# A Mamba-2 state recurrence inside a hybrid decoder layer: state packed chunk by chunk, stepped from PSUM

## The chip, the cores and the metric

One core of a Trainium2 chip runs the whole layer as one program. The metric is the device time of one execution in microseconds; shown is the median of several executions. The profile of one execution gives the times of single instructions on the engines: TensorE (PE, with its weight loads as PEld), VectorE (DVE), ScalarE (ACT), GpSimd (POOL) and SyncE (SP), which issues DMAs.

## What is computed

One decoder layer over 2048 tokens of width 1024. A joint input projection feeds two groups of heads: an RG-LRU group and a Mamba-2 SSD group; both outputs go through one output projection, and a SwiGLU feed-forward follows. The change lies in the SSD group alone. With 16 heads of 64 channels, a state of 128 and chunks of 128 tokens, the reference computes:

```
a_cs = jnp.cumsum(a, axis=-1)
Lmat = jnp.exp(segsum(a))
scores = jnp.einsum("bclgn,bcsgn->bgcls", Cm, Bm)
y_diag = jnp.einsum("bgecls,bcsgep->bclgep", scores[:, :, None] * Lmat, xs)
decay_states = jnp.exp(a_cs[..., -1:] - a_cs)
states = jnp.einsum("bclgn,bgecl,bclgep->bcgepn", Bm, decay_states, xs)
...
prev_states = jnp.einsum("bgezc,bcgepn->bzgepn", decay_chunk, states)[:, :-1]
y_off = jnp.einsum("bclgn,bcgepn,bgecl->bclgep", Cm, prev_states, jnp.exp(a_cs))
return (y_diag + y_off).reshape(b, t, g, e, p)
```

`prev_states` is a recurrence over chunks: the state ahead of chunk c+1 is the state ahead of chunk c, times the decay of chunk c, plus the chunk's own `states`.

## The kernel before

The sequence is cut in two blocks of 1024 tokens (NB = 2), a block in 8 chunks of 128 (NC = 8). Per block, a loop makes the projections of the input tile by tile: each tile of 128 columns is 48 matmuls of 128x512 (L133, L134, L135), since each fp32 product is made of three products of split operands (`s_hi`, `s_lo` for the weights, `hx` for the activations). Weights are loaded two tiles ahead through SP's queue (L208), rounded by ScalarE (L128) and their remainder taken by VectorE (L129).

The SSD group has 8 tiles `xi` per block, each with two heads (64 columns each), so there are 16 mixes (`ssd_mix`). For each tile `ssd_proj` makes the projections of x and z, with the convolution (L288 to L293) and SiLU (L473 for x, L478 for z). `ssd_mix` is a generator in three parts, which `site` runs between the projections of the next tile:

- Part one: transposes of x (L490), x times dt (`xd`, L492) and times the decay to the chunk's end (`xe`, L494), and the decay matrix `L` (L500 to L502).
- Part two: the states of the 8 chunks, 8 matmuls of 128x128 into one PSUM tile `pst` (L506). ScalarE copies the state from the block before (`sc`) and `pst` into a tile `U` whose chunks lie innermost, [state, column, 9] (L508, L509), and spreads the decays `aet` into a tile `AT` of the same shape (L511). VectorE runs one scan over all 1152 elements (L513), with decay 0 at the first of each nine. The state after the last chunk goes back to `sc` (L516, first block only). `L` is multiplied with the scores `SM` (L517).
- Part three: 8 matmuls with chunk c of `U` as the stationary operand and C as the moving one into `po` (L521), VectorE scales that (L522) and adds the skip (L523); 16 matmuls of the diagonal part into `py` (L527); then sum, gate, and spill to DRAM.

fp32 matmuls show as two passes each, so 8 matmuls are 16 instructions in the trace. PSUM tiles named `pq` come from a pool of two: the transposes L490 of the next mix write the buffer of `po`, which L522 empties. Working tiles `t4` come from a pool of nine. A scheduler places the instructions on the engines by priority in program order; each engine runs its own in order.

Of the kernel before, what the change touches and what calls it, by code (L numbers as in the profile page):

```python
# [8 lines left out]
F32 = mybir.dt.float32  # L9
F32R = mybir.dt.float32r  # L10
AF = mybir.ActivationFunctionType
ALU = mybir.AluOpType
# [3 lines left out]
P = 128  # L16
# [4 lines left out]
NB = T // TB  # L21
HB = 512
NC = TB // P
NH = 16
# [21 lines left out]
def hybrid_layer(ctx: ExitStack, tc: tile.TileContext, x, w_in, pack, heads, rows, wa, wx, w_out, w_gu, w_dn, out):  # L46
    nc = tc.nc
    v, a, te, g, sy = nc.vector, nc.scalar, nc.tensor, nc.gpsimd, nc.sync
# [20 lines left out]
    def par(n, i=0, w=None):  # L69
        o, full = PK[n]  # L70
        return pk[:, o + i:o + i + (w or 1)]
# [65 lines left out]
    def bc(ap, shape):  # L137
        return ap.broadcast_to(shape)

    # ------------------------------------------------ mixers  # L140
    mp = ctx.enter_context(ExitStack())
    pp = mp.enter_context(tc.tile_pool(name="pp", bufs=2, space=PSUM))
    pq = mp.enter_context(tc.tile_pool(name="pq", bufs=2, space=PSUM))
# [112 lines left out]
    with ExitStack() as fr:  # L256
        fc = fr.enter_context(tc.tile_pool(name="fc", bufs=1, reuse_waits="tile"))
        tl = fr.enter_context(tc.tile_pool(name="tl", bufs=1, reuse_waits="tile"))
        tp = fr.enter_context(tc.tile_pool(name="tp", bufs=1, reuse_waits="tile"))
# [11 lines left out]
        def t4(shape=(P, TB)):  # L271
            w = 1
            for n in shape[1:]:
                w *= n
            t = tl.tile([P, P * (NC + 1)], F32, name="t4", bufs=NT4)[:, :w]
            if len(shape) == 3:
                t = t.rearrange("p (a b) -> p a b", b=shape[2])
            elif len(shape) == 4:
                t = t.rearrange("p (a b c) -> p a b c", b=shape[2], c=shape[3])
            return t  # L280

        def wide(name):
            return tp.tile([P, 2, NC, P], F32, name=name, bufs=2)
# [12 lines left out]
        def spill(gt, kt, b):  # L296
            a.dma_start(out=g_dr[b * NC:(b + 1) * NC, :, kt, :].rearrange("c p t -> p c t"),
                        in_=gt.rearrange("p (c t) -> p c t", t=P))

        def accum(gt, sq, acc, first):  # L300
            if first:
                a.activation(out=acc, in_=gt, func=AF.Square)
            else:
                a.activation(out=sq, in_=gt, func=AF.Square)
                v.tensor_add(out=acc, in0=acc, in1=sq)
# [110 lines left out]
        def ssd_dt3(b, dt, dta):  # L416
            sh = [P, NC, NH]
            fl = "p c h -> p (c h)"
            pc = pq.tile([P, 2, 512], F32, name="pq")
            te.matmul(pc[:, 0, 0:P], lhsT=tri, rhs=dta.rearrange(fl), start=True, stop=True)  # L420
            te.matmul(pc[:, 1, 0:P], lhsT=ones, rhs=dta.rearrange(fl), start=True, stop=True)
            pr = pq.tile([P, TB], F32, name="pq")
            for c in range(NC):
                te.matmul(pr[0:NH, c * P:(c + 1) * P], lhsT=dta[:, c, :], rhs=tri, start=True, stop=True)
            cr = tp.tile([P, NC, P], F32, name="Bt", bufs=1).rearrange("p c l -> p (c l)")[0:NH, :]
            v.tensor_copy(out=cr, in_=pr[0:NH, :])
            sy.dma_start(out=cs_dr[b], in_=cr)
            cs = tp.tile(sh, F32, name="cs")
            a.copy(out=cs.rearrange(fl), in_=pc[:, 0, 0:P])
            ed = tp.tile(sh, F32, name="ed")  # L430
            v.tensor_tensor(out=ed.rearrange(fl), in0=pc[:, 1, 0:P], in1=cs.rearrange(fl), op=ALU.subtract)
            a.activation(out=ed, in_=ed, func=AF.Exp)
            aet = tp.tile([P, NH, NC + 1], F32, name="aet")
            v.memset(aet, 0.0)
            a.activation(out=aet[:, :, 1:], in_=pc[:, 1, 0:P].rearrange("p (c h) -> p h c", h=NH), func=AF.Exp)
            return dt, cs, ed, aet

        def ssd_group(b, gi, hT, between):
# [42 lines left out]
        def ssd_mix(b, xi, xc, sz, dts, grp, acc):  # L481
            dt, cs, ed, aet = dts
            C, Bt, SM = grp
            h0 = 2 * xi
            L = wide("L")
            for j in range(2):
                sy.dma_start(out=L[:, j].rearrange("p c l -> p (c l)"), in_=cs_dr[b, h0 + j].partition_broadcast(P))
            pt = pq.tile([P, NC, 2, 64], F32, name="pq")
            for c in range(NC):
                te.transpose(pt[:, c].rearrange("p j d -> p (j d)"), xc[:, c * P:(c + 1) * P], ident)  # L490
            xd = t4((P, NC, 2, 64))
            v.tensor_tensor(out=xd, in0=pt, in1=bc(dt[:, :, h0:h0 + 2, None], [P, NC, 2, 64]), op=ALU.mult)  # L492
            xe = t4((P, NC, 2, 64))
            v.tensor_tensor(out=xe, in0=xd, in1=bc(ed[:, :, h0:h0 + 2, None], [P, NC, 2, 64]), op=ALU.mult)  # L494
            er = t4()
            for j in range(2):
                sy.dma_start(out=er[64 * j:64 * j + 64, :], in_=cs_dr[b, h0 + j].partition_broadcast(64))
            a.activation(out=er, in_=er, func=AF.Exp)
            csb = bc(cs.rearrange("p c h -> p h c")[:, h0:h0 + 2, :, None], [P, 2, NC, P])
            v.tensor_tensor(out=L, in0=L, in1=csb, op=ALU.subtract)  # L500
            v.tensor_scalar(out=L, in0=L, scalar1=0.0, scalar2=None, op0=ALU.min)
            a.activation(out=L, in_=L, func=AF.Exp)  # L502
            yield
            pst = pq.tile([P, NC, P], F32, name="pq")
            for c in range(NC):
                te.matmul(pst[:, c, :], lhsT=Bt[:, c, :], rhs=xe[:, c].rearrange("p j d -> p (j d)"), start=True, stop=True)  # L506
            U = t4((P, P, NC + 1))
            a.copy(out=U[:, :, 0], in_=sc[:, xi, :])  # L508
            a.copy(out=U[:, :, 1:].rearrange("p d c -> p c d"), in_=pst)  # L509
            AT = t4((P, 2, 64, NC + 1))  # L510
            a.copy(out=AT, in_=bc(aet[:, h0:h0 + 2, None, :], [P, 2, 64, NC + 1]))  # L511
            Uf = U.rearrange("p d c -> p (d c)")
            v.tensor_tensor_scan(out=Uf, data0=AT.rearrange("p j d c -> p (j d c)"), data1=Uf,  # L513
                                 initial=0.0, op0=ALU.mult, op1=ALU.add)
            if b + 1 < NB:
                v.tensor_copy(out=sc[:, xi, :], in_=U[:, :, NC])  # L516
            v.tensor_tensor(out=L, in0=L, in1=bc(SM[:, None, :, :], [P, 2, NC, P]), op=ALU.mult)  # L517
            yield
            po = pq.tile([P, NC, P], F32, name="pq")
            for c in range(NC):  # L520
                te.matmul(po[:, c, :], lhsT=U[:, :, c], rhs=C[:, c * P:(c + 1) * P], start=True, stop=True)  # L521
            v.tensor_tensor(out=er, in0=po.rearrange("p c l -> p (c l)"), in1=er, op=ALU.mult)  # L522
            v.scalar_tensor_tensor(out=xc, in0=xc, scalar=par("sd", xi), in1=er, op0=ALU.mult, op1=ALU.add)  # L523
            py = pq.tile([P, NC, P], F32, name="pq")
            for c in range(NC):
                for j in range(2):
                    te.matmul(py[64 * j:64 * j + 64, c, :], lhsT=xd[:, c, j, :], rhs=L[:, j, c, :], start=True, stop=True)  # L527
            v.tensor_tensor(out=xc, in0=py.rearrange("p c l -> p (c l)"), in1=xc, op=ALU.add)
            v.tensor_mul(out=sz, in0=xc, in1=sz)
            spill(sz, 8 + xi, b)  # L530
            accum(sz, xe.rearrange("p c j d -> p (c j d)"), acc, xi == 0)
# [24 lines left out]
        sc = fc.tile([P, 8, P], F32, name="sc")  # L556
# [80 lines left out]
                while stages:  # L637
                    site(3)

    # ------------------------------------------------ output projection  # L640
    def build_op(b, o, halloc, ralloc=raw_tile):
        res = []
        for j in range(2):
            r = ralloc().rearrange("p (k c) -> p k c", c=HB)
            sy.dma_start(out=r, in_=h_dr[b][o][:, 2 * j:2 * j + 2, :])
            for k in range(2):
                hi, lo = halloc(), halloc()
                a.copy(out=hi, in_=r[:, k])
                v.tensor_sub(out=lo, in0=r[:, k], in1=hi.bitcast(F32))  # L649
                res.append((hi, lo))  # L650
        return res
# [26 lines left out]
    with ExitStack() as orr:  # L678
# [36 lines left out]
        for n, t in enumerate(tiles):  # L715
# [34 lines left out]
            b, i, j = t // NC, t % 4, (t % NC) // 4  # L750
# [3 lines left out]
                turn.append(lambda b=b, i=i, j=j, xnt=xnt: turned(b, i, j, xnt))  # L754
    mp.close()

    # ------------------------------------------------ FFN: gate and up
    pf = ctx.enter_context(tc.tile_pool(name="pf", bufs=8, space=PSUM, reuse_waits="tile"))

    def bank():  # L760
# [126 lines left out]
                    for o, z in ((4, s1), (2, s2), (3, s3), (6, s4)):  # L887
                        a.dma_start(out=f_dr[b][o][:, k, :], in_=z)

    # ------------------------------------------------ FFN: down  # L890
    hxs.close()
    with ExitStack() as fb:
        fd = fb.enter_context(tc.tile_pool(name="fd", bufs=1, reuse_waits="tile"))
# [90 lines left out]
        p = prod(0, list(range(2, KF, 2)) + [0], [(2, 0), (2, 1), (2, NB), (4, 0)])  # L984
# [3 lines left out]
        p = prod(2)  # L988
        for t in range(NT):
            v.tensor_add(out=u2[:, t], in0=p[t], in1=m1[:, t])  # L990
        p = prod(3)
        for t in range(NT):
            v.tensor_add(out=u3[:, t], in0=p[t], in1=u2[:, t])
        p = prod(4)
# [5 lines left out]
        p = prod(5)  # L1000
# [10 lines left out]
        p = prod(6)  # L1011
# [54 lines left out]
```

## Time and profile before

| | us |
|---|---|
| median of 3 runs | 2681.18 |
| lowest and highest | 2680.36, 2682.27 |
| span of the profiled execution | 2681.0 |
| TensorE busy in it | 2652.9 |
| VectorE busy | 1803.1 |
| ScalarE busy | 1190.1 |

The profiled execution is as long as the median run, so durations of its rows can be set against the times directly. Busy time of TensorE counts matmuls that overlap in the pipeline, so the chain of work that ended last and the list of waits are read beside it. The two SSD stretches lie at about 90 to 355 us and 600 to 870 us of the span.

### The profile page before, as it was taken

The page shows a single profiled execution, that of the slowest core. Times are in us where ns is not written, and L with a number is a line of the kernel's source. Part 1 is how long each engine was busy: PE and PEld are TensorE (multiplying, and loading weights), DVE is VectorE, ACT ScalarE, POOL GpSimd, SP SyncE. Part 2 cuts the span into 40 slices and gives each one's busy share as a digit, 9 for nine tenths or more (in the row PEclk, how much of TensorE's full clock was granted, in tenths as well). Part 3 has the DMA queues.
Part 4 walks back from the last instruction along what each step waited for, and adds up shares of the span by engine and source line. Part 5 has one row for each costly group of instructions (what it writes and reads, how often), then busy time and mean ns, then how long its engine had stood idle before and what let it go on. Part 6 is the DMA issues. An engine that isn't in the chain of part 4 may idle for free.

```text
span 2681.0 us, 31808 instructions
## 1 busy us (share of the span) xinstructions
PE 2652.9 (99%) x12416; PEld 2206.0 (82%) x12416; DVE 1803.1 (67%) x2460; ACT 1190.1 (44%) x1408; POOL 1.1 (0%) x8
## 2 busy tenths in 40 slices
PE   7999999999999999999999999999999999999998
PEld 5888888878888888888887888888888888888887
DVE  7676777777767777644468776768676766334576
ACT  6554567765554668422244222224222223322443
POOL 0000000000000000000000000000000000000000
PEclk9999999999999999999999999999999999999999
DMA  4333353133223633634355423335333234444664
GB/s 151 103 97 99 94 171 131 47 97 112 91 79 110 210 120 126 227 127 141 130 181 171 151 83 114 103 114 184 111 106 107 96 105 159 147 153 138 220 244 138
DMA packets 186775, 354.39 MB, mean 132 GB/s; under 512 B 18400, under 2 KB 91232, under 8 KB 186624
## 3 DMA queue, kind: packets, MB, share of 16 engines
q1 hardware_dynamic: 85712, 253.16, 28.9%
q10 hardware_dynamic: 100912, 99.20, 10.7%
q8 instruction: 98, 1.61, 0.2%
q14 instruction: 53, 0.43, 0.0%
HBM read 250.45 MB, written 101.84 MB: 131 GB/s over the span
## 4 chain that ended last, share of the span: by engine, by line
PE 94%; DVE 3%; ACT 2%; issue 1%; DMA 1%; SPq 0%; DVEq 0%; ACTq 0%
PE pf L135 16%; PE pf L133 16%; PE pf L134 16%; PE pp L133 11%; PE pp L134 11%; PE pp L135 11%; PE pq L134 3%; PE pq L133 3%; PE pq L135 3%; PE pq L521 2%; PE pq L527 1%; PE pq L506 1%; PE pq L490 1%; PE pq L692 0%; DVE lx L293 0%
## 5 line engine op out<-in xcount | busy, mean ns | idle before, releaser
L133 PE MATMUL pp<-hx,s_hi 128*128 128x512 f32 x1408 | 555.0, 394 | 0.0
L135 PE MATMUL pp<-hx,s_lo 128*128 128x512 f32 x1408 | 551.0, 391 | 0.0
L134 PE MATMUL pp<-hx,s_hi 128*128 128x512 f32 x1408 | 550.3, 391 | 0.6 <-DVE hx L239 0.6
L128 ACT CAST s_hi<-raw 128x1024 fp32r<-128x1024 f32 (+1 forms) x167 | 170.4, 1024 | 318.9 <-PE pq L134 95.0
L135 PEld LDWEIGHTS pp<-hx,s_lo 128*128 128x128 f32 x1408 | 264.9, 188 | 55.8 <-issue 0.2
L134 PEld LDWEIGHTS pp<-hx,s_hi 128*128 128x128 f32 x1408 | 265.3, 188 | 54.7 <-DVE hx L239 1.0
L133 PEld LDWEIGHTS pp<-hx,s_hi 128*128 128x128 f32 x1408 | 265.2, 188 | 54.0 <-issue 0.3
L133 PE MATMUL pf<-hx,s_hi 128*128 128x512 f32 x704 | 274.2, 389 | 0.5 <-ACT s_hi L128 0.5
L135 PE MATMUL pf<-hx,s_lo 128*128 128x512 f32 x704 | 273.9, 389 | 0.7 <-DVE s_lo L129 0.7
L134 PE MATMUL pf<-hx,s_hi 128*128 128x512 f32 x704 | 273.9, 389 | 0.0
L129 DVE TENSOR_TENSOR s_lo<-raw,s_hi 128x1024 fp32r<-128x1024 f32 (+1 forms) x167 | 198.1, 1188 | 97.6 <-ACT s_hi L128 92.3
L909 DVE TENSOR_TENSOR d_lo<-draw,d_hi 128x1024 fp32r<-128x1024 f32 (+1 forms) x110 | 121.4, 1129 | 170.3 <-ACT d_hi L908 170.0
L128 ACT CAST s_hi<-S 128x1024 fp32r<-128x1024 f32 x86 | 90.3, 1050 | 266.6 <-PE pf L134 233.2
L908 ACT CAST d_hi<-draw 128x1024 fp32r<-128x1024 f32 (+1 forms) x110 | 104.8, 980 | 212.4 <-PE pf L134 175.5
L134 PE MATMUL pf<-d_lo,d_hi 128*128 128x512 f32 x504 | 196.1, 389 | 0.0
L135 PE MATMUL pf<-d_hi,d_lo 128*128 128x512 f32 x504 | 195.9, 389 | 0.0
L133 PE MATMUL pf<-d_hi 128*128 128x512 f32 x504 | 194.6, 389 | 0.0
L135 PEld LDWEIGHTS pf<-hx,s_lo 128*128 128x128 f32 x704 | 132.1, 188 | 29.0 <-DVE s_lo L129 1.6
L133 PEld LDWEIGHTS pf<-hx,s_hi 128*128 128x128 f32 x704 | 132.1, 188 | 28.1 <-ACT s_hi L128 0.9
L134 PEld LDWEIGHTS pf<-hx,s_hi 128*128 128x128 f32 x704 | 132.1, 188 | 27.4
L293 DVE SCALAR_TENSOR_TENSOR lx<-xr,pk,lx 128x1024 f32<-128x1024 f32 x108 | 138.2, 1280 | 16.3 <-ACT lx L290 15.4
L134 PE MATMUL pf<-hy,s_hi 128*128 128x512 f32 x356 | 138.8, 390 | 1.5 <-DVE hy L649 1.4
(321 smaller groups left out, 4586.6 us busy)
## 6 DMA issues: line engine op xcount, KB each, us to landing
raw<-w_gu_dram SPq DMA_DIRECT2D x86, 512.0 KB, 4.1
f_dr<-fo ACTq DMA_DIRECT2D x154, 256.0 KB, 4.3
raw<-w_in_dram SPq DMA_DIRECT2D x74, 512.0 KB, 3.3
draw<-f_dr SPq DMA_DIRECT2D x57, 512.0 KB, 4.4
L<-cs_dr SPq DMA_DIRECT2D x32, 512.0 KB, 5.1
g_dr<-t ACTq DMA_DIRECT2D x32, 512.0 KB, 3.6
raw<-g_dr SPq DMA_DIRECT2D x32, 512.0 KB, 4.9
raw<-h_dr SPq DMA_DIRECT2D x26, 512.0 KB, 4.5
```

The costliest lines, as they stand in the source:

```text
L128: a.copy(out=hi, in_=raw)
L129: v.tensor_sub(out=lo, in0=raw, in1=hi.bitcast(F32))
L133: te.matmul(o, lhsT=wh, rhs=hi, start=start, stop=False)
L134: te.matmul(o, lhsT=wh, rhs=lo, start=False, stop=False)
L135: te.matmul(o, lhsT=wl, rhs=hi, start=False, stop=stop)
L293: v.scalar_tensor_tensor(out=y, in0=xr[:, k:k + TB], scalar=cw(k), in1=y, op0=ALU.mult, op1=ALU.add)
L490: te.transpose(pt[:, c].rearrange("p j d -> p (j d)"), xc[:, c * P:(c + 1) * P], ident)
L506: te.matmul(pst[:, c, :], lhsT=Bt[:, c, :], rhs=xe[:, c].rearrange("p j d -> p (j d)"), start=True, stop=True)
L521: te.matmul(po[:, c, :], lhsT=U[:, :, c], rhs=C[:, c * P:(c + 1) * P], start=True, stop=True)
L527: te.matmul(py[64 * j:64 * j + 64, c, :], lhsT=xd[:, c, j, :], rhs=L[:, j, c, :], start=True, stop=True)
L908: a.copy(out=hi, in_=r)
L909: v.tensor_sub(out=lo, in0=r, in1=hi.bitcast(F32))
```

## The change

`U` is laid out chunk by chunk, [state, chunk, column], and holds the states after each chunk. VectorE makes it in 16 steps of 128x64, one for each chunk and head: the state before times the head's decay of the chunk (a scalar for each partition) plus the chunk's part, read from PSUM. The copies of `sc` and `pst` into `U`, the spread decays `AT` and the scan are gone; `aet` loses its zero column and the memset. The matmuls of part three read chunk c-1 of `U`, and `sc` for chunk 0. The copy back to `sc` moves behind these matmuls and to ScalarE.

```diff
-            aet = tp.tile([P, NH, NC + 1], F32, name="aet")
-            v.memset(aet, 0.0)
-            a.activation(out=aet[:, :, 1:], in_=pc[:, 1, 0:P].rearrange("p (c h) -> p h c", h=NH), func=AF.Exp)
+            aet = tp.tile([P, NH, NC], F32, name="aet")
+            a.activation(out=aet, in_=pc[:, 1, 0:P].rearrange("p (c h) -> p h c", h=NH), func=AF.Exp)
...
-            U = t4((P, P, NC + 1))
-            a.copy(out=U[:, :, 0], in_=sc[:, xi, :])
-            a.copy(out=U[:, :, 1:].rearrange("p d c -> p c d"), in_=pst)
-            AT = t4((P, 2, 64, NC + 1))
-            a.copy(out=AT, in_=bc(aet[:, h0:h0 + 2, None, :], [P, 2, 64, NC + 1]))
-            Uf = U.rearrange("p d c -> p (d c)")
-            v.tensor_tensor_scan(out=Uf, data0=AT.rearrange("p j d c -> p (j d c)"), data1=Uf,
-                                 initial=0.0, op0=ALU.mult, op1=ALU.add)
-            if b + 1 < NB:
-                v.tensor_copy(out=sc[:, xi, :], in_=U[:, :, NC])
+            U = t4((P, NC, P))
+            for c in range(NC):
+                for j in range(2):
+                    q = slice(64 * j, 64 * j + 64)
+                    v.scalar_tensor_tensor(out=U[:, c, q], in0=(sc[:, xi, q] if c == 0 else U[:, c - 1, q]),
+                                           scalar=aet[:, h0 + j, c:c + 1], in1=pst[:, c, q],
+                                           op0=ALU.mult, op1=ALU.add)
...
-                te.matmul(po[:, c, :], lhsT=U[:, :, c], rhs=C[:, c * P:(c + 1) * P], start=True, stop=True)
+                te.matmul(po[:, c, :], lhsT=(sc[:, xi, :] if c == 0 else U[:, c - 1, :]),
+                          rhs=C[:, c * P:(c + 1) * P], start=True, stop=True)
+            if b + 1 < NB:
+                a.copy(out=sc[:, xi, :], in_=U[:, NC - 1, :])
```

Behind the change the line numbers shift by a few: the scaling L522 is L521 there, the matmuls L521 are L517, L527 is L526, the transposes L490 are L489, the SiLU L473 is L472, the steps are L510.

On TensorE, the third mix of the first block, at the end of a projection (the last three rows of which are shown first). Before (`t_1256` is U, `Cc` is C):

```order
L133 MATMUL pp<-hx,s_hi 128x512
L134 MATMUL pp<-hx,s_hi 128x512
L135 MATMUL pp<-hx,s_lo 128x512
L521 MATMUL pq<-Cc,t_1256 128x128 x8
L527 MATMUL pq<-L,t_1181 64x128 x16
L490 MATMUL pq<-ident,lx 128x128 x8
L133 MATMUL pp<-hx,s_hi 128x512
```

Now (`t_1277` is U):

```order
L133 MATMUL pp<-hx,s_hi 128x512
L134 MATMUL pp<-hx,s_hi 128x512
L135 MATMUL pp<-hx,s_lo 128x512
L517 MATMUL pq<-Cc,sc 128x128
L517 MATMUL pq<-Cc,t_1277 128x128 x7
L526 MATMUL pq<-L,t_1202 64x128 x16
L489 MATMUL pq<-ident,lx 128x128 x8
L133 MATMUL pp<-hx,s_hi 128x512
```

The place is the same, and the first of the eight reads `sc`. Between the matmuls of the states (L506, now L505) and this group stand 48 projection matmuls in both.

On VectorE, the same mix, from the decay matrix to the scaling of `po`. Before:

```order
L517 TENSOR_TENSOR L<-L,SM 128x2048
L513 SCALAR_TENSOR_TENSOR t_1256<-t_1259,t_1256 128x1152
L291 COPY halo<-xr 128x3
L293 SCALAR_TENSOR_TENSOR lx<-xr,pk,lx 128x1024
L516 COPY sc<-t_1256 128x128
L293 SCALAR_TENSOR_TENSOR lx<-xr,pk,lx 128x1024
L129 TENSOR_TENSOR s_lo<-raw,s_hi 128x1024
L293 SCALAR_TENSOR_TENSOR lx<-xr,pk,lx 128x1024
L287 COPY xr<-halo 128x3
L129 TENSOR_TENSOR s_lo<-raw,s_hi 128x1024
L522 TENSOR_TENSOR t_1185<-pq,t_1185 128x1024
```

Now:

```order
L513 TENSOR_TENSOR L<-L,SM 128x2048
L510 SCALAR_TENSOR_TENSOR t_1277<-sc,aet,pq 128x64 x2
L510 SCALAR_TENSOR_TENSOR t_1277<-t_1277,aet,pq 128x64 x14
L291 COPY halo<-xr 128x3
L293 SCALAR_TENSOR_TENSOR lx<-xr,pk,lx 128x1024
L129 TENSOR_TENSOR s_lo<-raw,s_hi 128x1024
L293 SCALAR_TENSOR_TENSOR lx<-xr,pk,lx 128x1024 x2
L287 COPY xr<-halo 128x3
L129 TENSOR_TENSOR s_lo<-raw,s_hi 128x1024
L521 TENSOR_TENSOR t_1206<-pq,t_1206 128x1024
```

The sixteen steps stand where the scan (L513 of before) stood; the copy to `sc` is gone from this queue, and the rest keeps its place but for one weight remainder.

On ScalarE, the same mix, from the decay matrix on. Before:

```order
L502 ACTIVATE L<-L 128x2048
L288 COPY xr<-pp 128x1024
L509 COPY t_1256<-pq 128x8x128
L290 ACTIVATE lx<-pp,pk 128x1024
L128 CAST s_hi<-raw 128x1024
L473 ACT_TABLE_LOAD
L473 ACTIVATE lx<-lx 128x1024
L128 CAST s_hi<-raw 128x1024
L478 ACTIVATE t_1362<-pp 128x1024
```

Now:

```order
L501 ACTIVATE L<-L 128x2048
L288 COPY xr<-pp 128x1024
L290 ACTIVATE lx<-pp,pk 128x1024
L128 CAST s_hi<-raw 128x1024 x2
L472 ACT_TABLE_LOAD
L472 ACTIVATE lx<-lx 128x1024
L520 COPY sc<-t_1277 128x128
L477 ACTIVATE t_1394<-pp 128x1024
```

The copy out of PSUM is gone, the second weight cast stands ahead of the SiLU of x, and the copy to `sc` stands between the two SiLUs.

## Rows read from the trace of the kernel before

**Rows 1.** Page: busy time by engine, and the chain's shares.
```profile
PE 2652.9 (99%) x12416; PEld 2206.0 (82%) x12416; DVE 1803.1 (67%) x2460; ACT 1190.1 (44%) x1408; POOL 1.1 (0%) x8
...
PE 94%; DVE 3%; ACT 2%; issue 1%; DMA 1%; SPq 0%; DVEq 0%; ACTq 0%
```
**Rows 2.** Waits of TensorE: who waited for whom, us, times, longest.
```profile
PE pq L165 <- DVE rs_v L89: 9.5, 1, 9.5
...
PE pq L490 <- DVE t L522: 0.7, 1, 0.7
```
**Rows 3.** Weight loads by line: ns minimum/median/maximum, first and last start.
```profile
L521 PEld LDWEIGHTS pq<-Cc,t x256: 319/335/341, 110.7 to 865.8; 128*128 128x128 f32 x128
...
L506 PEld LDWEIGHTS pq<-t,Bt x256: 187/192/192, 98.0 to 851.3; 128*128 128x128 f32 x128
...
L462 PEld LDWEIGHTS pq<-Cc,lx x64: 187/192/192, 69.9 to 731.0; 128*128 128x128 f32 x64
```
**Rows 4.** Chain, third mix: start us, us on the chain, what.
```profile
158.90 1.78 PE pq L506 x16
...
171.63 3.70 PE pq L521 x16
```
**Rows 5.** Timeline of TensorE, first mix: start us, us, instruction, count.
```profile
98.21 1.95 PE L506 MATMUL pq<-t,Bt 128*128 128x128 f32 x16
99.91 0.48 PE L133 MATMUL pp<-hx,s_hi 128*128 128x512 f32 x1
...
110.93 3.86 PE L521 MATMUL pq<-Cc,t 128*128 128x128 f32 x16
114.72 1.97 PE L527 MATMUL pq<-L,t 128*64 128x128 f32 x32
116.62 1.09 PE L490 MATMUL pq<-ident,lx 128*128 128x128 f32 x8
```
**Rows 6.** Timeline of VectorE, third mix; idle time before in brackets.
```profile
159.37 2.29 DVE L517 TENSOR_TENSOR L<-L,SM 128x2048 f32<-128x2048 f32 x1 [1.98 <-ACT L L502]
162.88 2.56 DVE L513 TENSOR_TENSOR_SCAN t<-t,t 128x1152 f32<-128x1152 f32 x1 [1.22 <-ACT t L509]
165.35 0.14 DVE L291 COPY halo<-xr 128x3 f32<-128x3 f32 x1
...
170.44 0.17 DVE L287 COPY xr<-halo 128x3 f32<-128x3 f32 x1
172.51 1.23 DVE L129 TENSOR_TENSOR s_lo<-raw,s_hi 128x1024 fp32r<-128x1024 f32 x1 [1.90 <-ACT s_hi L128]
175.37 1.23 DVE L522 TENSOR_TENSOR t<-pq,t 128x1024 f32<-128x1024 f32 x1 [1.63 <-PE pq L521]
```
**Rows 7.** Timeline of ScalarE, third mix.
```profile
160.72 2.12 ACT L509 COPY t<-pq 128x1024 f32<-128x1024 f32 x1 [0.49 <-PE pq L506]
...
170.44 1.06 ACT L473 ACTIVATE lx<-lx 128x1024 f32<-128x1024 f32 x1 [4.38 <-DVE lx L293]
171.43 1.04 ACT L128 CAST s_hi<-raw 128x1024 fp32r<-128x1024 f32 x1
```
**Rows 8.** Copy of the decays, ScalarE: ns minimum/median/maximum.
```profile
L511 ACT COPY t<-aet x16: 1136/1138/1195, 93.9 to 845.7; 128x1152 f32<-128x1152 f32 x16
```
**Rows 9.** VectorE: timeline of short and dependent instructions; then two shapes by line.
```profile
55.09 0.28 DVE L105 TENSOR_TENSOR sp<-sp 128x128 f32<-128x128 f32 x1
55.29 1.22 DVE L129 TENSOR_TENSOR s_lo<-raw,s_hi 128x1024 fp32r<-128x1024 f32 x1
...
116.09 1.28 DVE L523 SCALAR_TENSOR_TENSOR lx<-lx,pk,t 128x1024 f32<-128x1024 f32 x1
117.48 1.23 DVE L528 TENSOR_TENSOR lx<-pq,lx 128x1024 f32<-128x1024 f32 x1
...
L169 DVE SCALAR_TENSOR_TENSOR hx<-pq,pk,hx x32: 726/747/752, 14.7 to 553.1; 128x512 fp32r<-128x512 f32 x32
...
L293 DVE SCALAR_TENSOR_TENSOR lx<-xr,pk,lx x108: 1256/1280/1292, 48.8 to 1043.8; 128x1024 f32<-128x1024 f32 x108
```

## The prediction

> **What bounds the kernel now.** I read the page's busy times and its chain first. TensorE is busy for 2652.9 of 2681.0 us and 94% of the chain that ended last is its work [rows 1]. A page can show a busy engine that is really waiting between pipelined matmuls, so the second view is who TensorE waited for: 9.5 us once, at the very start for the first norm, and after that only short ones; the one in this stage is 0.7 us, at L490 for VectorE's L522 [rows 2]. So whatever shortens TensorE's own work shortens the kernel, and what ScalarE or VectorE do counts only when it makes TensorE wait.
>
> The third view is the price of the matmuls of one mix. The 128 matmuls of L521 read the state U as stationary operand, one chunk being every ninth fp32 word. Each is two passes, and a weight load of a pass takes 335 ns. The matmuls of L506 and L462 have the same size (128x128, fp32), read contiguous operands, and their weight loads take 192 ns; L462 streams C as L521 does, so the moving operand is not what makes L521 slow [rows 3]. In the chain, the 16 passes of L521 take 3.70 us and the 16 of L506 1.78 us [rows 4].
>
> **TensorE's part of the change.** U becomes [chunk, column], so chunk c is 128 contiguous words, and chunk 0 reads `sc`, contiguous too. The count of matmuls is the same: 8 per mix, the first now from another tile. If the stride is what costs, L521 falls to L506's time: 3.70 - 1.78 = 1.92 us a mix by the chain's pieces [rows 4]. By starts, L521 holds TensorE for 114.72 - 110.93 = 3.79 us and L506 for 99.91 - 98.21 = 1.70 us, a difference of 2.09 us [rows 5]; the starts leave out that the matmul just behind L506 still runs long (0.48 us), so I take 1.92 and keep 2.09 as the other end. 16 mixes, all on the chain: 16 x 1.92 = 30.7 us (to 33.4 us).
>
> The trace shows only 192 and 335 ns at the same 128 columns [rows 3]. [...]
>
> **ScalarE's part.** Three copies go: a short one of `sc` into U, that of the states out of PSUM (2.12 us) and that of the decays (1.14 us) [rows 7, 8]. That is over 3.2 us a mix, more than 52 us in all, off an engine that does not bound; I count it as nothing. One copy of the last state to `sc` comes in half of the mixes, in place of VectorE's. It must wait for the first matmul of L521, which reads `sc`; queued behind it on ScalarE are the SiLU of z and the next weight cast, neither of which TensorE needs before the projection after next. What could matter is a cast that moves: in the third mix the second cast of weights (L128) stood behind the SiLU of x (L473), now it stands ahead of it. That cast sometimes waits for TensorE to end the projection; it takes 1.04 us, the SiLU 1.06 us [rows 7]. So the SiLU can end some 2.1 us after the projection, and its reader, the transposes of L490, come only after L521 and L527, 1.78 + 1.90 = 3.7 us after it [rows 4, 5]. Cost nothing; without that cover at most 12 x 1 us. SP's queue gets a weight load one or two places later in a few mixes. The weights are loaded two projections ahead, and one projection holds TensorE from 99.91 to 110.93 [rows 5]; these 22 us hide it.
>
> **VectorE's part.** The scan goes: 165.35 - 162.88 = 2.47 us from its start to the next [rows 6], and with it the wait for ScalarE's copy. Half the mixes also lose a copy of the state. Sixteen steps of 128x64 come. No row has this shape. The same operation takes 747 ns for 512 elements from PSUM and 1280 ns for 1024 from SBUF [rows 9], so 1.04 ns an element and 214 ns fixed, thus about 280 ns for 64. What counts is the distance between starts. A short one with a next that doesn't wait for it gives way after 0.20 us (55.09 to 55.29) though it lasts 0.28; an instruction that waits for the one just before starts 0.11 us after its end (116.09 + 1.28 to 117.48) [rows 9]. Each step waits for the step two before it (the other head's step stands between), so 0.21 us is my value; the ends are 0.17 us (half of 0.28 and a little) and 0.39 us (0.28 + 0.11, as if each waited for the one just before). Sixteen cost 3.4 us (2.7 to 6.2) in place of the scan's 2.47.
>
> Does TensorE wait for that? Take the third mix. VectorE starts L517 at 159.37 and is free for the next at about 161.6; the states are there by then, since L506 ends at 158.90 + 1.78 = 160.68 [rows 4, 6]. Steps at 0.21 end at 165.0, against 165.35 for the scan. L521 starts at about 171.4, and would do so in the changed kernel by the same distance from L506. The state is 6 us early; only steps above 0.6 us make L521 itself wait.
>
> The tighter path is VectorE's queue up to L522, since the transposes L490 write the PSUM buffer that L522 empties. Behind the steps stand 165.35 to 170.44, 5.1 us, less the copy that leaves, then L287 (0.17), a weight remainder L129 (1.23) and L522 (1.23) [rows 6]. With steps of s, L522 ends at 161.6 + 16 s + 4.9 + 0.17 + 1.23 + 1.23 = 169.1 + 16 s. TensorE would reach L490 at about 171.4 + 1.78 + 1.90 = 175.1. The new anchor costs 0.4 us: L129 waits for a cast that waits for the end of the projection (171.43, then 172.51, [rows 6, 7]), so it ends some 2.2 us after the projection, and L522 can no longer start right at L521's end, 1.8 us after it. That leaves 169.1 + 16 s < 174.7, so s up to 0.35 us costs nothing. With 0.21 there are 2.2 us of slack. The 0.7 us wait of [rows 2] shows one mix in which this path already ends last; it may stay or grow towards 2 us, and I count it as unchanged.
>
> **Sum.** 2681.0 - 30.7 = 2650.3 us of span. The median of the runs shown is 0.2 us above the span, so 2650.5; I say 2650. Two bounds: 33.4 instead of 30.7, with the 0.7 us and some of the other short waits gone, 2644 to 2647; a microsecond lost in each of the twelve mixes in which L490 follows directly, 2662.
>
> **The rivals.**
> The steps cost part of the gain. For it: the instruction form was never seen at this size, it has a wait on its own engine each time, and its operand is in PSUM. Against it: the slack of 2.2 us. At the upper end of 0.39 us a step VectorE is 16 x 0.04 = 0.6 us late in each of twelve mixes, and 2650 becomes 2658; at 0.42, 2664. Chance 0.16.
>
> The stride is not the cause. Then L521 keeps 3.70 us, VectorE's and ScalarE's work changes under cover, and the time is 2681, give or take 3. [...] Chance 0.06.
>
> VectorE becomes the bound (slower). One mechanism: steps that wait for the full write of the step before. Past 0.35 us each further 0.1 us costs 1.6 us a mix. At 0.35 + 1.92 / 16 = 0.47 us the gain is gone; from 0.50 us on the kernel is slower by more than 0.2%; at 0.6 us it is about 16 x (0.25 x 16 - 1.92) = 33 us slower, 2714. The price of such a wait, 0.39 us with the gap of [rows 9], speaks against it. Chance 0.04.
>
> **How the numbers follow.** The forecast, full gain and no new wait of note (2644 to 2655), has 0.74; part of the gain 0.16; no gain 0.06; slower 0.04. A range of 2644 to 2662 takes in the forecast and the nearer half of the second case, about 0.82. The boundary of 0.2%, 5.4 us, is about what a measurement of this kernel can tell from no change. Faster by more: 0.74 + 0.16 = 0.90. Within it: 0.06. Slower by more: 0.04.
>
> **What would show it.** Weight loads of the line that was L521 at 192 ns and its 16 passes at 1.78 us in the chain confirm the main term; 335 ns refutes it. The sixteen steps should span 3.4 us, and the L490 group should wait for VectorE no more than 1 or 2 us in all. If L490 waits in most mixes with VectorE named, the step price was wrong; if the projections wait for s_hi or s_lo, the moved casts or weight loads were underrated. If the weight loads fall and the span does not, the gain went into a wait that the TensorE list will name.

## The result, and the profile after

The changed kernel takes 2649.94 us (median, 2647.66 to 2652.0), beside 2680.77 us for the kernel before on the same chip: a ratio of 0.9883, 95% interval 0.987 to 0.9896, or 30.8 us less. The profiled execution spans 2650.1 us at a granted clock of 0.998, that of the kernel before 2681.0 us: the spans differ by 30.9 us, as the medians do, so the rows of the two can be set against each other. It was forecast at 2650.

Beside the lines named with the change, the chunk states are now L505 (before L506), the product of `L` and `SM` L513 (L517) and the copy back to `sc` L520 (L516).

First the page: busy time by engine, and the shares of the chain. They answer to [rows 1].

```profile
PE 2621.2 (99%) x12416; PEld 2174.4 (82%) x12416; DVE 1808.6 (68%) x2690; ACT 1137.9 (43%) x1368; POOL 1.1 (0%) x8
...
PE 93%; DVE 3%; ACT 2%; issue 1%; DMA 1%; DVEq 0%; ACTq 0%; SPq 0%
```

TensorE has as many instructions as before and 2652.9 - 2621.2 = 31.7 us less to do, which is the whole gain within 1 us. ScalarE lost 52.2 us and VectorE gained 5.5 us; neither shows in the time.

Next the price of one instruction, by line: nanoseconds minimum, median and maximum, then the first and last start. The first two rows answer to L521 of [rows 3], the third is the new step.

```profile
L517 PEld LDWEIGHTS pq<-Cc,t x224: 190/192/192, 109.7 to 834.5; 128*128 128x128 f32 x112
...
L517 PEld LDWEIGHTS pq<-Cc,sc x32: 187/190/193, 109.4 to 832.9; 128*128 128x128 f32 x32
...
L510 DVE SCALAR_TENSOR_TENSOR t<-t,aet,pq x224: 272/275/279, 99.3 to 825.0; 128x64 f32<-128x64 f32 x112
```

The weight loads of the state fell from 335 to 192 ns, the price of the contiguous lines. In the chain of the third mix (start, microseconds on the chain, what) the 16 passes weigh what those of the chunk states weigh, 1.79 us where [rows 4] has 3.70:

```profile
153.74 1.78 PE pq L505 x16
...
166.46 1.79 PE pq L517 x16
```

What TensorE waited for (total, times, longest) shows the price paid for it. In this stage it is one line, which answers to the second of [rows 2].

```profile
PE pq L489 <- DVE t L521: 1.3, 1, 1.3
```

It is one wait of 1.3 us where there was one of 0.7. How near a mix without a wait comes to one is read from the timelines of the third (start, duration, instruction; in brackets the idle time before it and who ended it). VectorE, as in [rows 6]:

```profile
150.25 2.29 DVE L499 TENSOR_TENSOR L<-L,cs 128x2048 f32<-128x2048 f32 x1 [2.79 <-DMA L<-cs_dr]
...
156.85 2.29 DVE L513 TENSOR_TENSOR L<-L,SM 128x2048 f32<-128x2048 f32 x1 [2.03 <-ACT L L501]
159.06 0.47 DVE L510 SCALAR_TENSOR_TENSOR t<-sc,aet,pq 128x64 f32<-128x64 f32 x2
159.44 2.77 DVE L510 SCALAR_TENSOR_TENSOR t<-t,aet,pq 128x64 f32<-128x64 f32 x14
162.13 0.16 DVE L291 COPY halo<-xr 128x3 f32<-128x3 f32 x1
...
167.34 1.23 DVE L129 TENSOR_TENSOR s_lo<-raw,s_hi 128x1024 fp32r<-128x1024 f32 x1
168.49 1.22 DVE L521 TENSOR_TENSOR t<-pq,t 128x1024 f32<-128x1024 f32 x1
```

ScalarE, as in [rows 7], and TensorE's transposes behind both:

```profile
166.26 1.05 ACT L128 CAST s_hi<-raw 128x1024 fp32r<-128x1024 f32 x1 [6.51 <-PE pp L134]
167.33 1.28 ACT L472 ACT_TABLE_LOAD   x1
168.62 1.06 ACT L472 ACTIVATE lx<-lx 128x1024 f32<-128x1024 f32 x1
```

```profile
170.08 1.09 PE L489 MATMUL pq<-ident,lx 128*128 128x128 f32 x8
```

The sixteen steps take 162.13 - 159.06 = 3.07 us, 0.192 us each. The scaling ends at 169.71 and the SiLU at 169.68, both some 0.4 us before the transposes start at 170.08. TensorE does not wait in this mix, but there is little left.

### The profile page after: what moved, and what is told of

The parts are those of the page before. It is cut to its first block, busy times and chain, and to the rows that moved or that the text cites. A ratio compares the mean times of both kernels' runs of the same rounds, so it can differ in the third digit from the quotient of the medians.

```text
span 2650.1 us, 31981 instructions
## 1 busy us (share of the span) xinstructions
PE 2621.2 (99%) x12416; PEld 2174.4 (82%) x12416; DVE 1808.6 (68%) x2690; ACT 1137.9 (43%) x1368; POOL 1.1 (0%) x8
## 4 chain that ended last, share of the span: by engine, by line
PE 93%; DVE 3%; ACT 2%; issue 1%; DMA 1%; DVEq 0%; ACTq 0%; SPq 0%
PE pf L135 16%; PE pf L134 16%; PE pf L133 16%; PE pp L133 11%; PE pp L135 11%; PE pp L134 11%; PE pq L133 2%; PE pq L134 2%; PE pq L135 2%; PE pq L505 1%; PE pq L526 1%; PE pq L517 1%; PE pq L489 1%; PE pq L165 0%; PE pq L691 0%
```

## The experiments

The theory: the gain is the weight loads of the state, whose price hangs on the layout of the stationary operand; the steps, the missing copies and the moved casts cost or bring TensorE nothing. The rivals: the steps or the copies bring a part of it; or VectorE's queue takes a part of it away. All ratios are to the kernel before, with 95% intervals.

### The steps with the old layout, and the old scan with the new layout

The first kernel keeps the steps and undoes only the packing: chunk c is again every ninth word.

```diff
-            U = t4((P, NC, P))
+            U = t4((P, P, NC + 1))
+
+            def Uc(c):
+                return U[:, :, c]
...
-                    v.scalar_tensor_tensor(out=U[:, c, q], in0=(sc[:, xi, q] if c == 0 else U[:, c - 1, q]),
+                    v.scalar_tensor_tensor(out=Uc(c)[:, q], in0=(sc[:, xi, q] if c == 0 else Uc(c - 1)[:, q]),
...
-                te.matmul(po[:, c, :], lhsT=(sc[:, xi, :] if c == 0 else U[:, c - 1, :]),
+                te.matmul(po[:, c, :], lhsT=(sc[:, xi, :] if c == 0 else Uc(c - 1)),
...
```

> Undoes the packing alone: the sixteen steps stay, but U is again laid out with its chunks innermost, every ninth word, so the matmuls of chunks 1 to 7 load weights with a stride and chunk 0 still reads the packed sc. Theory (the stride of the weight load is the whole gain): the strided loads go back from 192 to about 335 ns, 7 of 8 matmuls a mix lose their share of 1.92 us, so 16 x 7/8 x 1.92 = 27 us come back and the time is about 2677 against 2650. Rival (the gain comes from the queues: no copies on ScalarE, no scan): the time stays near 2650 and the loads read 192 ns.

Measured: 2676.7 us, ratio 0.9986 (0.9977 to 0.9996). The weight loads by line, those of `U` and those of `sc` in the same group of matmuls:

```profile
L521 PEld LDWEIGHTS pq<-Cc,t x224: 312/335/341, 110.1 to 860.2; 128*128 128x128 f32 x112
...
L521 PEld LDWEIGHTS pq<-Cc,sc x32: 187/190/193, 109.8 to 857.0; 128*128 128x128 f32 x32
...
L514 DVE SCALAR_TENSOR_TENSOR t<-t,aet,pq x224: 315/335/358, 99.6 to 849.8; 128x64 f32<-128x64 f32 x112
```

With the stride back, the gain is gone but for 4 to 5 us. Of those, 16 x 1.92 / 8 = 3.8 us are chunk 0, which reads the contiguous `sc` at 190 ns. The steps are slower too, since they read and write the strided state (335 ns, last row), but TensorE's list of waits has no line of this stage, and its busy time is back at 2648.2 us: the loss is in the loads. With the same slow loads, steps and scan are worth the same. This shows the layout as the cause.

The second kernel is the converse: the kernel before, scan and copies as they were, with one more ScalarE copy that packs the state for the matmuls.

```diff
+            Up = AT.rearrange("p j d c -> p (j d c)")[:, 0:NC * P].rearrange("p (c d) -> p c d", d=P)
+            a.copy(out=Up, in_=U[:, :, 0:NC].rearrange("p d c -> p c d"))
...
-                te.matmul(po[:, c, :], lhsT=U[:, :, c], rhs=C[:, c * P:(c + 1) * P], start=True, stop=True)
+                te.matmul(po[:, c, :], lhsT=Up[:, c, :], rhs=C[:, c * P:(c + 1) * P], start=True, stop=True)
```

> The other half alone: the copies, the spread decays and the scan of the kernel before stay, and ScalarE makes one more copy, of the scanned state into a packed tile from which the eight matmuls load their weights. Theory (packing alone is the gain, and it doesn't matter how the state is made as long as TensorE doesn't wait): loads at 192 ns, time 2650 give or take 3, although ScalarE does about 16 x 1.9 = 30 us more than before. Rival (the shorter path through VectorE and ScalarE matters too): the extra copy makes the transposes or the state matmuls wait in the mixes, and the time lies between 2655 and 2670.

Measured: 2665.13 us, ratio 0.9939 (0.9924 to 0.9954). My theory, the full gain, fell, and the time lies where the rival put it: half of the gain came. The weight loads are at 192 ns, so the rest went into waits. TensorE's, in its list:

```profile
PE pq L490 <- DVE t L524: 9.5, 6, 2.5
...
PE pq L456 <- DVE halo L291: 2.3, 2, 1.2
```

These are 11.8 us where the changed kernel has 1.3, and the two profiled spans (2660.3 and 2650.1) differ by 10.2. The chain ahead of the longest of these waits, in order of time:

```profile
113.32 7.57 DMA L<-cs_dr
120.99 2.30 DVE L L500
...
129.67 2.01 ACT t L509
131.70 2.56 DVE t L513
...
140.17 1.04 ACT s_hi L128
...
142.37 1.23 DVE t L524
143.74 1.06 PE pq L490 x8
```

A transfer, the decay matrix, ScalarE's copy of the states out of PSUM (L509), the scan (L513), the convolution, the weight cast and its remainder, and only then the scaling L524 that empties the buffer of the transposes. The packing copy I added (L518, 2.21 us) is not on this chain; in the chain of the two SSD stretches L509 stands six times and L518 never. All the rest is the order of the kernel before, whose list has one wait of 0.7 us here [rows 2] and where each strided group of matmuls took 1.92 us longer. So in the mixes that wait the path to the scaling is the bound; that the longer group covered it in the kernel before is concluded from that one short wait, not tried.

### How far a stride may go

Two kernels lay the state in pairs or in fours of chunks, so that a chunk is every second or every fourth word. The first of them (the second has 4 for each 2):

```diff
-            U = t4((P, NC, P))
+            U = t4((P, NC // 2, P, 2))
+
+            def Uc(c):
+                return U[:, c // 2, :, c % 2]
...
-                te.matmul(po[:, c, :], lhsT=(sc[:, xi, :] if c == 0 else U[:, c - 1, :]),
+                te.matmul(po[:, c, :], lhsT=(sc[:, xi, :] if c == 0 else Uc(c - 1)),
...
```

> As the changed kernel, but two chunks interleaved word by word, so a weight load takes every second word. Theory A (a load pays as soon as its words are not neighbours): about 335 ns and some 2677 us. [...]

> As the run with every second word, but four chunks interleaved, every fourth word. [...] A third possibility, that the price grows with the stride, expects something between 192 and 335 ns here, some 2660 us, and less at every second word.

Measured: every second word 2649.95 us, ratio 0.9883 (0.9868 to 0.9898); every fourth 2676.39 us, 0.9981 (0.9971 to 0.9991). The weight loads of the first, then of the second kernel:

```profile
L521 PEld LDWEIGHTS pq<-Cc,t x224: 196/196/198, 109.6 to 832.6; 128*128 128x128 f32 x112
```

```profile
L521 PEld LDWEIGHTS pq<-Cc,t x224: 307/330/331, 109.8 to 861.9; 128*128 128x128 f32 x112
```

The price is a step, not a slope: 192 ns for each word, 196 for every second, 330 for every fourth, 335 for every ninth. The step lies between 8 bytes (196 ns) and 16 (330 ns). Theory A, a slow load as soon as the words are not neighbours, fell at every second word; the third possibility, a price that grows with the stride, fell at every fourth, where nearly the whole of it is paid already. Why the step lies there no run shows.

### More steps, and ScalarE's copies brought back

The next kernel doubles the number of steps, 32 of 128x32, to see how much VectorE's queue can take.

```diff
-                for j in range(2):
-                    q = slice(64 * j, 64 * j + 64)
+                for z in range(4):
+                    j, q = z // 2, slice(32 * z, 32 * z + 32)
```

> The changed kernel with each of the sixteen steps cut in two of 128x32, so 32 steps a mix that do the same. At 0.19 us a step measured for 64 columns, and 0.033 us less for half of them, 32 take about 5.1 us instead of 3.1: 2.0 us a mix more on VectorE, nothing more on TensorE. The scheduler also puts the next transposes 3 to 9 projection matmuls later on TensorE (0.7 to 2.0 us). Theory (the slack of 2.2 us that the prediction worked out for the queue up to the scaling is there): the time stays at 2650 give or take 2. Rival (the slack is gone, since the trace of the changed kernel shows the scaling ending 0.4 us ahead of the transposes): about 1 us is lost in each of twelve mixes, 2660, and the transposes wait for VectorE in most of them.

Measured: 2657.23 us, ratio 0.9906 (0.9892 to 0.9921), between the two expectations. The price of a step by line, VectorE's timeline of the third mix, and two lines of TensorE's waits:

```profile
L510 DVE SCALAR_TENSOR_TENSOR t<-t,aet,pq x448: 236/240/246, 98.8 to 830.0; 128x32 f32<-128x32 f32 x150
```

```profile
158.37 0.72 DVE L510 SCALAR_TENSOR_TENSOR t<-sc,aet,pq 128x32 f32<-128x32 f32 x4
...
163.44 0.16 DVE L291 COPY halo<-xr 128x3 f32<-128x3 f32 x1
```

```profile
PE pq L134 <- DVE t L363: 2.1, 1, 2.1
...
PE pq L489 <- DVE xr L287: 1.0, 1, 1.0
```

The 32 steps take 163.44 - 158.37 = 5.07 us, 2.0 us more than the sixteen, and the time grows by 7.3 us. But the wait that the rival named is missing: the transposes L489 wait once, and not for the scaling. The scheduler placed them some matmuls later in this kernel; in the third mix the scaling ends at 171.48 and they start at 172.62. Nor does most of the loss lie in the mixes. Of the 7.2 us by which the profiled span is longer, the stretches from the first to the last chunk states (L505) of the two blocks hold 0.7 and 1.2 us (225.06 beside 224.38, 224.10 beside 222.93); 1.8 us lie between the blocks and 4.3 us behind the start of the last chunk states, less 0.7 us by which the first ones start earlier. Behind the last mix TensorE waits 2.1 us for L363, which belongs to the RG-LRU heads, and the granted clock from 890 to 925 us is 0.95; in the changed kernel it is 1.00 there (883 to 918 us). So this run doesn't price the path to the scaling; how the longer queue on VectorE leads to the loss outside the mixes is open.

Then the changed kernel with two ScalarE copies that nobody reads, of about the size of those that the change removed, the longer one with their strided write:

```diff
+            UD = t4((P, P, NC + 1))
+            a.copy(out=UD[:, :, 1:].rearrange("p d c -> p c d"), in_=U)
+            a.copy(out=UD.rearrange("p (j d) c -> p j d c", j=2)[:, :, :, 0:NC], in_=bc(aet[:, h0:h0 + 2, None, :], [P, 2, 64, NC]))
```

> The changed kernel with two copies of the old kind put back on ScalarE as work whose result nobody reads: the state, reordered, and the spread decays, about 3.2 us a mix in ScalarE's queue behind the first weight cast. Theory (ScalarE's relief is worth nothing, as the prediction counted it): 2650 give or take 2. Rival (the SiLU of x is nearly late in the changed kernel, since its table load now stands behind the weight cast): the copies, which wait for the steps, push the SiLU and with it the transposes; 1 us in each of twelve mixes gives 2662, and TensorE's list of waits names the SiLU.

Measured: 2648.96 us, ratio 0.9879 (0.9862 to 0.9895). The longer of the copies by line (the other takes 1056 ns):

```profile
L514 ACT COPY t<-t x16: 2187/2217/2232, 101.1 to 821.3; 128x1024 f32<-128x1024 f32 x16
```

ScalarE has its 52 us back (1189.9 us busy) and the time does not move. What the change takes off ScalarE's total is worth nothing here. What it takes off the path to the scaling is another matter, which the next two kernels ask.

### A copy ahead of the steps, packed and strided

The first lets ScalarE copy the states out of PSUM into a packed tile, which the steps read; the second makes the same copy with the layout of the kernel before, chunks innermost.

```diff
+            S = t4((P, NC, P))
+            a.copy(out=S, in_=pst)
...
-                                           scalar=aet[:, h0 + j, c:c + 1], in1=pst[:, c, q],
+                                           scalar=aet[:, h0 + j, c:c + 1], in1=S[:, c, q],
```

```diff
+            S = t4((P, P, NC + 1))
+            a.copy(out=S[:, :, 1:].rearrange("p d c -> p c d"), in_=pst)
...
-                                           scalar=aet[:, h0 + j, c:c + 1], in1=pst[:, c, q],
+                                           scalar=aet[:, h0 + j, c:c + 1], in1=S[:, q, c + 1],
```

> The changed kernel, but ScalarE first copies the chunk states from PSUM into a packed tile, in order, and the steps read that copy, as the scan had to. TensorE's work is that of the changed kernel. The copy takes about 1.0 us and stands behind the convolution's copy in ScalarE's queue, so the steps start some 1 to 2 us later. Theory (with packed loads the way through VectorE has little slack, and the 15 us that the scan with packed loads lost went into the wait for ScalarE's copy): 2656 to 2665, with the transposes waiting for VectorE in several mixes. Rival (that run lost its time to the scan's own length or to its extra copy): 2650 give or take 2.

> The kernel after, with ScalarE's long copy of before put back on the path: it copies the states out of PSUM into a tile whose chunks lie innermost, as in the kernel before (2.1 us with the strided write there), and the sixteen steps read that tile in place of PSUM and write the packed state. So the path to the state holds the same copy as in the kernel with the scan and an added packing copy; the scan and its order of work are missing. If the 2.1 us copy ahead of VectorE is what that kernel lost, this one loses a part of it too: 2656 to 2662 us, with TensorE's transposes waiting for VectorE's scaling in several mixes. If the copy is covered, 2650 to 2653 us with at most 2 us of such waits, and the loss belongs to the scan's own order of work, in which the convolution and the weight cast stand behind the exponential of the decay matrix. The steps read every ninth word; I expect 275 to 335 ns each.

Measured: with the packed copy 2651.82 us, ratio 0.9888 (0.9871 to 0.9904); with the strided copy 2659.96 us, 0.9917 (0.9901 to 0.9934). The order of the instructions is the same on every engine; they differ in the layout of the copy and of the operand that the steps read. The copy and the steps of the packed one by line, and what VectorE's idle time ahead of the steps was for (total, times):

```profile
L508 ACT COPY t<-pq x16: 1010/1014/1017, 99.0 to 822.6; 128x1024 f32<-128x1024 f32 x16
...
L512 DVE SCALAR_TENSOR_TENSOR t<-t,aet,t x224: 276/280/290, 100.8 to 826.6; 128x64 f32<-128x64 f32 x112
...
  ACT t L508: 4.4, 4
```

The same of the strided one (there who waited for the copy), and TensorE's wait:

```profile
L508 ACT COPY t<-pq x16: 2097/2136/2162, 99.5 to 831.0; 128x1024 f32<-128x1024 f32 x16
...
  DVE t L512: 17.5, 16
...
L512 DVE SCALAR_TENSOR_TENSOR t<-t,aet,t x224: 317/335/400, 102.2 to 836.9; 128x64 f32<-128x64 f32 x112
```

```profile
PE pq L489 <- DVE t L523: 4.7, 5, 3.1
```

For the packed copy my theory (2656 to 2665) fell: 1.0 us of copy is covered, and TensorE's list has no wait of this stage. For the strided one it held: a copy of 2.1 us, for which VectorE waits in all 16 mixes, and steps of 335 ns in place of 280 cost 8.1 us more, while the weight loads are at 192 ns in both. So the path from the chunk states to the scaling has room for the copy of 1.0 us, and not for the one of 2.1 us with sixteen steps that take 4.03 us in place of 3.13 (second mix). The kernel with the scan and the packing copy has the same strided copy in the chain of its waits, and no slow steps (its scan takes 2.56 us), yet it lost 5 us more. So the copy is on the path there, but how much of that loss is the copy's, the scan's or that of ScalarE's order, in which the convolution's copy stands behind the exponential of the decay matrix, is not separated. A scan that writes the packed layout itself wasn't tried.

No kernel of these is faster than the changed one beyond the intervals; those with every second word, with the copies that nobody reads and with the packed copy equal it within them.

## Why the prediction was right, and where its steps were off

**The main term.** 16 x (3.70 - 1.78) = 30.7 us was forecast, 30.8 us was measured in the median, and both halves are in the rows: loads of 192 ns, 16 passes in 1.79 us. The other end, 33.4 us by starts, was wrong for the reason given there. The rival in which the stride is not the cause fell: a load of the same 128 columns takes 192 ns in the changed kernel and 335 ns in the first experiment, and the two differ in the layout of the state alone.

**ScalarE's total** was rightly counted as nothing: with 52 us put back the time stayed.

**The price of a step** was 0.21 us by estimate and 0.192 us measured; a step was to last 280 ns and lasts 275. So waiting for the step two before it added nothing that shows: 0.192 us between starts is no more than the 0.20 us of a pair in [rows 9] that doesn't wait. The sixteen span 3.07 us, 3.4 were forecast.

**VectorE's slack** was mis-sized, though nothing came of it. The sum gave 2.2 us before the scaling would delay the transposes; in the third mix 0.37 us are left. It took from the trace of before that VectorE starts the product of `L` and `SM` 0.5 us after TensorE starts the chunk states [rows 4, 6]. In the changed kernel it starts 156.85 - 153.74 = 3.1 us after: VectorE waits 2.79 us for its transfer at L499 (0.45 us at L500 in the kernel before, 152.82 us), and that wait is passed on. In both kernels the two transfers are issued right behind the diagonal matmuls; between 138 and 153 us, which holds this issue in both, they land after 4.7 us (median of the two, out<-in, count, KB each, us from issue to landing) before and after 6.6 us in the changed kernel:

```profile
L<-cs_dr SPq DMA_DIRECT2D x2, 512.0 KB, 4.7
```

```profile
L<-cs_dr SPq DMA_DIRECT2D x2, 512.0 KB, 6.6
```

Over the whole kernel VectorE's waits for these transfers grow from 9.7 us to 23.7. Why they take longer no run shows. The threshold fell with it: the prediction let steps of up to 0.35 us cost nothing, but with 0.37 us left it is by estimate nearer 0.192 + 0.37 / 16 = 0.215 us in this mix. No run here tests it, since the kernel with 32 half steps has its transposes later and they do not wait for the scaling. The rival in which the steps cost part of the gain was nearer than 2.2 us of slack made it. That no wait of note came of the mis-sized slack is luck, as far as this sum goes: the late transfer happened to use up a little less than all of it.

**The moved cast** was given 1.6 us of cover: a SiLU that ends 2.1 us behind the projection, and transposes 3.7 us behind it. The sum left out the table load of 1.28 us that now stands between the cast and the SiLU. In the third mix the cast starts at 166.26, the SiLU ends at 169.68, 3.4 us later, and 0.4 us of cover are left. The claim that it costs nothing held in this mix by little.

**The wait of the transposes** was to stay at 0.7 us or grow towards 2; it is 1.3 us, in one mix.

**The scan and its copies** were counted as beside the bound in the kernel before, and they were. What the prediction did not say is that they would have been the bound without the strided loads: the packing with the scan left in place, in the one form tried (one more copy), gives half of the gain. The steps bring nothing of their own, as the first experiment shows, but with them all of the packing comes through.

## To carry to other kernels

An fp32 stationary operand that is read at every ninth word made a group of matmuls twice as long here (3.70 us in place of 1.78), and no wait in TensorE's list shows it: compare the weight loads line by line at the same size, and lay the operand out so that neighbouring words, or every second one (192 and 196 ns a load here, 330 at every fourth), belong to one load. Before a saving on the bounding engine is booked in full, follow the path that ends at its next instruction from the other engines, with its transfers and table loads, and ask how much of it the slow work was hiding. Where that path is too long, shorten it in the same change; relief of an engine's total elsewhere was worth nothing here.

## What the runs showed of the hardware

A stride of 36 bytes slows VectorE's short steps too: 335 ns in place of 275 with the output and the state that is read strided (the first kernel), and 335 in place of 280 with one input strided (the last). ScalarE's copy of 128x1024 out of PSUM takes 1014 ns with a packed output and 2136 ns with one of 36-byte stride.

In the kernel with the scan and the packing copy, matmuls ran slower for a while behind TensorE's longest wait for the scaling (2.5 us). The stretches around it, with the busy time of each engine, then the granted clock, the share of the DMA engines and GB/s:

```profile
141.20:143.70 2.50, 0.06 (x2) 0.00 (x0) 2.44 (x3) 1.23 (x2) 0.00 (x0) 1.00 0.15 21
143.70:146.00 2.30, 2.26 (x12) 2.00 (x13) 2.19 (x2) 0.00 (x0) 0.00 (x0) 0.73 1.00 315
146.00:150.00 4.00, 4.00 (x15) 3.20 (x14) 3.64 (x4) 1.05 (x2) 0.00 (x0) 0.73 1.00 288
150.00:160.00 10.00, 10.00 (x54) 8.57 (x53) 6.86 (x4) 7.12 (x7) 0.00 (x0) 1.00 0.26 71
```

TensorE stands idle for 2.5 us, and behind that the granted clock is 0.73 up to 150 us and 1.00 after it. Matmuls of 128x512 follow each other there at 0.43 us (144.95, 145.38) until about 148, and behind 148.28 at 0.23. The nine slow ones make some 9 x 0.2 = 1.8 us on top of the 2.5. In the same stretch of the changed kernel, which has no wait there, the granted clock is 1.00. Not every wait of this size is followed by such a fall: behind two of 2.3 us in the same kernel (ending at 648.2 and 818.9 us) the granted clock stays at 1.00. Behind the 3.1 us wait of the kernel with the strided copy it is 0.63 (647.4 to 652.0 us).

```profile
144.95 0.63 PE L134 MATMUL pp<-hx,s_hi 128*128 128x512 f32 x1
145.38 0.63 PE L135 MATMUL pp<-hx,s_lo 128*128 128x512 f32 x1
...
148.28 0.39 PE L133 MATMUL pp<-hx,s_hi 128*128 128x512 f32 x1
```
